# One ring of 24 buffers for weights, late FFN features, q and k and pooled features in a two-layer hybrid trunk, and a queue order at the start

## The chip, the cores and the metric

The kernel runs on one core of one Trainium2 chip. The metric is the device time of one execution in microseconds (us). The engines are PE (TensorE: matmuls, with weight loads as PEld), DVE (VectorE), ACT (ScalarE), POOL (GpSimd) and SP (SyncE, which here only issues DMAs). Each engine works through its own queue in order.

## The reference, cut to what matters

Two layers on x of 512 x 1024 in float32. Each layer is a half-step FFN, a mixer and a second half-step FFN, each followed by a layer norm of the sum with the scaled input. The mixer of layer 0 is an attention of 8 heads, that of layer 1 a pooling mixer.

```python
def swiglu(x, w_gu, w_down):
    g, u = jnp.split(x @ w_gu, 2, axis=-1)
    return (jax.nn.silu(g) * u) @ w_down
...
    for i in range(DEPTH):
        x = layer_norm(DEEPNORM_ALPHA * x + 0.5 * swiglu(x, ffn_w_gu[i, 0], ffn_w_down[i, 0]), ln_g[i, 0], ln_b[i, 0])
...
        x = layer_norm(DEEPNORM_ALPHA * x + y, ln_g[i, 1], ln_b[i, 1])
        x = layer_norm(DEEPNORM_ALPHA * x + 0.5 * swiglu(x, ffn_w_gu[i, 1], ffn_w_down[i, 1]), ln_g[i, 2], ln_b[i, 2])
```

The inner width of an FFN is 2816. So there are six phases: FFN 0, attention, FFN 2, FFN 3, pooling, FFN 5 (the numbers are those of the layer norms behind them).

## The kernel before

Every product is done in three passes on two float32r halves of each operand (`mm3`, L99): high times low, high times high, low times high. `split` (L94) makes the halves: ACT copies the high one (L96), DVE subtracts for the low one (L97). Weights are split too, 458 times 128 x 1024.

The weights flow through one list of pieces and one list of units, written down before the first instruction. A **piece** is a load of 128 x 1024 (4 KB in each partition); a **unit** is one split of a piece. `load` (L179) puts a piece into one of RAW = 7 buffers "raw", with a DMA that SP issues. `prepare` (L192) splits the next unit into one of PARTS = 5 buffers "hi" and one of 5 "lo". `run_ahead` (L203) keeps 5 units prepared beyond those whose matmuls are written, and `load_ahead` (L188) keeps 7 pieces loaded. Both are called by `retire` (L213), which stands behind the matmuls that use a unit.

Most products of an FFN are done by a scheme with seven products in place of eight. A `Quad` (L128) has five pieces, of which two, s1 and s3, are sums of two blocks of weights: SP loads the first block, then POOL issues a DMA that adds the second one (L185). From the seven units of a quad, in the order `LATER` = 1, 2, 6, 5, 7, 3, 4, unit 6 is split from a sum which DVE makes: `sums` (L136) adds s1 to p11 and then p11 to p12 (both L139). Unit 4 of the whole list is the first of the first quad, so unit 6 of the whole list is the first with such a sum.

An FFN begins with four plain units (the first 256 columns of gate and up, L525 to L541): columns of rows 0 to 255 (h = 0) and then of rows 256 to 511 (h = 1). During h = 0, behind the third and the sixth stretch of 12 matmuls (`LATE`, L58), it takes up what is left of the layer norm before (`late`): the tiles t = 2 and t = 3 are transposed on PE (L312), brought from PSUM by ACT or DVE (L315, L323, L321), and split (L255 or L272). Behind h = 0 the input's own sums follow (`Seven.sums`, L282: four of `form`, L279). Then come ten quads jj (L548 to L580), whose gated features go to hT, 22 tiles of 128 x 512; then the down product, first by the same scheme for the features 0 to 7, then plainly (`BProduct`, L413), where `act` (L609) splits the other 14 features of hT in pairs. At the kernel's very start the second of the two `late` steps (L843) also calls `run_ahead`.

A mixer begins with `halves` (L390): blocks of 12 matmuls go through the first halves of up to four pairs of units, then through the second halves.

What sets the order: PE's instructions stay in the order of the program (L87). On the other engines the framework that builds the kernel orders the queues by its own estimate of when each instruction could start; among those that it takes to be ready, the one written first goes first. A buffer of a ring is given out again when its last reader is done.

Of the kernel before, what the change touches and what calls it, by code (L numbers as in the profile page):

```python
# [25 lines left out]
F32 = mybir.dt.float32  # L26
F32R = mybir.dt.float32r
AF = mybir.ActivationFunctionType
ALU = mybir.AluOpType
# [3 lines left out]
P = 128  # L33
S = 512
# [4 lines left out]
NF = FF // P  # L39
# [3 lines left out]
H = 8  # L43
DH = D // H
BUCKETS = 32
# [3 lines left out]
GW = 640  # L49
WINDOWS = (2, 4, 8, 16)  # L50
BLOCK = 8
R = 4
R_LAST = 5
RAW = 7
PARTS = 5
ACT = 7
# [23 lines left out]
def trunk(ctx, tc, x, rel_bias, ln_g, ln_b, w_gu, w_dq, w_down, a_in, a_out, b_in, b_group, b_scale, b_out, onehot, out):  # L80
    nc = tc.nc
# [92 lines left out]
    b_plain(b_out[0], POOL_ORDER)  # L174
    ffn_units(1, 1)

    parts, taken, retired = [], [0], [0]

    def load():  # L179
        p = pieces[len(loaded)]  # L180
        p.tile = wp.tile([P, 1024], F32, tag="raw", bufs=RAW, name=f"raw{len(loaded)}")
        dst = p.tile.rearrange("p (k c) -> p k c", c=p.src.shape[-1]) if len(p.src.shape) == 3 else p.tile
        nc.sync.dma_start(dst, p.src)
        if p.plus is not None:
            nc.gpsimd.dma_start(p.tile, p.plus, accum_op=ALU.add)  # L185
        loaded.append(p)

    def load_ahead():  # L188
        while len(loaded) < len(pieces) and (len(loaded) < RAW or pieces[len(loaded) - RAW].uses == 0):
            load()  # L190

    def prepare():  # L192
        i = len(parts)
        make, done = units[i]
        src = make()
        hi = wp.tile([P, 1024], F32R, tag="hi", bufs=PARTS, name=f"hi{i}")
        lo = wp.tile([P, 1024], F32R, tag="lo", bufs=PARTS, name=f"lo{i}")
        split(hi, lo, src)
        for p in done:
            p.uses -= 1  # L200
        parts.append((hi, lo))

    def run_ahead():  # L203
        load_ahead()
        while len(parts) < min(len(units), retired[0] + PARTS):
            prepare()
            load_ahead()

# [4 lines left out]
    def retire(count=1):  # L213

        retired[0] += count
        run_ahead()
# [44 lines left out]
    class Seven(Plain):  # L261
# [7 lines left out]
        def put(self, t, half, src):  # L269
            c = slice((t % 2) * P, (t % 2 + 1) * P)  # L270
            o = self.operand(((1, 2), (8, 3))[t // 2][half])
            split(o[:, 0, :, c], o[:, 1, :, c], src)  # L272

        def take(self, i, src):
            o = self.operand(i)
# [98 lines left out]
    def load_residual():  # L374
        if residual[0][1] is not None:
            row[:] = ln_params(residual[0][1])
# [93 lines left out]
    gd = dram.tile([H, GW], F32, name="gd")  # L470
    gr = dram.tile([H, P, GW], F32, name="gr")

    def bias_rows(room):

        oh, gs, rb = room[0:BUCKETS, 0:GW], room[0:H, 1024:1024 + GW], room[0:BUCKETS, 2048:2048 + H]
        nc.gpsimd.dma_start(oh, onehot)
        nc.gpsimd.dma_start(rb, rel_bias)
        gp = bank(6, "gp")
        nc.tensor.matmul(gp[:H, :], rb, oh[:, 0:512], start=True, stop=True)
# [13 lines left out]

    def ffn(n, x, dest):
        with tc.tile_pool(name=f"ffn{n}", bufs=1) as fp:
            hT = fp.tile([P, NF, S], F32, name=f"hT{n}")
            kept = {}

            def two(ap):
                return ap.rearrange("p (s c) -> p s c", c=256)  # L500
# [8 lines left out]
            def gate(f, t0, t1, g, u, sign):  # L509
                sg = fp.tile([P, t1 - t0], F32, tag=f"sg{t1 - t0}", bufs=1 if t1 - t0 == S else 2, name=f"sg{n}_{f}_{t0}")  # L510
                nc.scalar.activation(sg, g, AF.Silu, scale=sign)
                return nc.vector.scalar_tensor_tensor(hT[:, f, t0:t1], u, sign, sg, op0=ALU.mult, op1=ALU.mult)

            def product(acc, w, xi, first, last, shared=True):

# [12 lines left out]
            for h, xi in enumerate(((1, 2), (8, 3))):  # L528
                c = slice(h * 256, (h + 1) * 256)
                for i in range(4):  # L530
                    two_accs = [acc[:, c] for acc in accs[i // 2 * 2:i // 2 * 2 + 2]]
                    for _ in product(two_accs, w[i], x.parts[xi[i % 2]], i % 2 == 0, i % 2 == 1, False):
                        if steps in LATE:
                            late.pop(0)()
                        steps += 1
                    if h == 1:
                        if i % 2 == 1:
                            gate(i // 2, 0, S, accs[i - 1], accs[i], 1.0)
                        retire()
                if h == 0:  # L540
                    x.sums()  # L541

# [5 lines left out]
            for jj in QUADS:  # L548
                if n == 0 and jj == 2:
                    columns()  # L550
                if n == 0 and jj == 4:
                    bias_rows(hT[:, 14:22, :].rearrange("p f c -> p (f c)"))
                if jj == 2:
                    load_residual()
                ca = fp.tile([P, 2, S], F32, tag="ca", name=f"ca{n}_{jj}")
                cb = fp.tile([P, 2, 256], F32, tag="cb", name=f"cb{n}_{jj}")
                banks = [bank(i, f"gu{n}_{jj}_{i}") for i in (2 * ((jj + 1) % 3), 2 * ((jj + 1) % 3) + 1, 6 + jj % 2)]
# [51 lines left out]
            def act(f):  # L609
                if f // 2 not in pairs:  # L610
                    two = glob.tile([P, 2, 2, S], F32R, tag="act", bufs=ACT, name=f"h{n}_{f // 2}")
                    split(two[:, 0], two[:, 1], hT[:, f // 2 * 2:f // 2 * 2 + 2, :])
                    pairs[f // 2] = two
                two = pairs[f // 2]
                return two[:, 0, f % 2, :], two[:, 1, f % 2, :]
# [6 lines left out]


    def attention(n, x, dest):
        with tc.tile_pool(name="att", bufs=1) as ap:
            oT, qk, v, probs, pT = {}, {}, {}, {}, {}

            def project(acc, nm, h):
                two = [ap.tile([P, S], F32R, tag=f"{nm}{i}", bufs=2, name=f"{nm}{i}_{h}") for i in range(2)]
                split(two[0], two[1], acc)  # L630
                qk[nm, h] = two

            def values(hp, vp, tt):
                acc = bank(tt, f"v{hp}_{tt}")
# [63 lines left out]
            for hp in range(H // 2):  # L698
# [29 lines left out]
                values(hp, vp, 1)  # L728
                retire(2)
                transposes(h)  # L730
            out_p = BProduct(n, NK, lambda f: (oT[f // 2][:, 0, f % 2, :], oT[f // 2][:, 1, f % 2, :]), 1.0, dest)
            pre = [out_p.take(f) for f in range(NK - R)]
            for t in (1, 0, 3, 2):
# [7 lines left out]


    def pooling(n, x, dest):
        with tc.tile_pool(name="pool", bufs=1) as pp:
            inv = pp.tile([P, 16], F32, name="inv")
            sc = cols[:, 2 * NL:]
# [5 lines left out]
            def pool(acc, cc):  # L752
# [13 lines left out]
                                               op0=ALU.mult, op1=ALU.subtract)  # L766
                g = cc // 2
                if g not in pT:
                    pT[g] = [pp.tile([P, 2, S], F32R, tag=f"pT{i}_{g % 3}", name=f"pT{i}_{g}") for i in range(2)]
                return split(pT[g][0][:, cc % 2, :], pT[g][1][:, cc % 2, :], pl)  # L770

            def group(g, w, b0):
# [38 lines left out]
            def y_of(f):  # L811
                cc = POOL_ORDER[f]
                return yT[cc // 2][:, 0, cc % 2, :], yT[cc // 2][:, 1, cc % 2, :]

            out_p = BProduct(n, NK, y_of, 1.0, dest)
            pre = [out_p.take(f) for f in range(NK - R)]
            for t in range(NT):
# [66 lines left out]
```

## Time and profile before

| | |
|---|---|
| Time before, median of 3 runs | 1738.93 us (1737.85 to 1741.2) |
| The profiled execution, its own time | 1737.85 us |
| Its span, first to last instruction | 1736.1 us |
| PE busy | 1705.0 us (98% of the span) |
| DVE busy, ACT busy | 1251.3 us (72%), 825.6 us (48%) |
| Granted TensorE clock, mean | 0.997 |

The profile is of one execution. In its timeline a row has the start, the length, the engine, the line, the operation, its output and inputs, and in brackets how long the engine had sat idle before it and what ended that. In its list of waits a row says who waited for whom, for how many us in total, how many times, and the longest of these.

### The profile page before, as it was taken

Reading aid. Unit: us, or ns where it says so; the run is one execution under the profiler, and the core shown is the slowest. Engines: PE = TensorE matmul, PEld = TensorE weight load, DVE = VectorE, ACT = ScalarE, POOL = GpSimd, SP = SyncE. Lnnn points to the kernel's source line nnn. Section 1 sums busy time; section 2 is a strip of 40 time slices with the busy share of each in tenths; the row PEclk is TensorE's granted clock in tenths of the full one; section 3 lists DMA queues with packets and bytes.
Section 4 is the critical chain, followed back from the end, with each engine's and each line's share of the span. In section 5 each row is a group of like instructions: output and inputs, shape, how many; then the busy total and the mean of one; then the engine's idle time right before and its main releaser. Section 6 shows DMA issues by size and latency. Waiting matters only on the chain.

```text
span 1736.1 us, 28083 instructions
## 1 busy us (share of the span) xinstructions
PE 1705.0 (98%) x11555; PEld 1585.1 (91%) x11555; DVE 1251.3 (72%) x1657; ACT 825.6 (48%) x1161; POOL 94.5 (5%) x132
## 2 busy tenths in 40 slices
PE   7999999999999999999999999999999999999998
PEld 6999998889888899999888999998888899999886
DVE  5777698266665877878928778788279787877946
ACT  5545464254443555455525554564254454545620
POOL 1010000000000000000000000000000000000000
PEclk9999999999999999999999999999999999999999
DMA  6787756323221376666633666756223356776611
GB/s 209 188 238 186 189 146 209 97 74 110 86 86 51 109 194 176 185 181 164 194 97 85 183 182 185 184 154 197 96 88 106 99 166 187 185 189 180 185 62 49
DMA packets 84864, 257.30 MB, mean 148 GB/s; under 512 B 8128, under 2 KB 25576, under 8 KB 84736
## 3 DMA queue, kind: packets, MB, share of 16 engines
q1 hardware_dynamic: 70080, 202.40, 35.0%
q0 software_dynamic: 14656, 53.12, 17.1%
q8 instruction: 90, 1.47, 0.3%
q14 instruction: 38, 0.31, 0.1%
HBM read 253.37 MB, written 4.74 MB: 149 GB/s over the span
## 4 chain that ended last, share of the span: by engine, by line
PE 93%; DMA 3%; DVE 2%; issue 1%; ACT 0%; SPq 0%; DVEq 0%; POOLq 0%
PE gu L101 16%; PE gu L102 16%; PE gu L103 16%; PE acc L102 8%; PE acc L103 8%; PE acc L101 8%; DMA raw<-in_ffn_w_gu 2%; PE qk L103 2%; PE da L102 2%; PE da L101 2%; PE da L103 2%; PE qk L101 2%; PE qk L102 2%; PE d L102 1%; PE d L103 1%; PE d L101 1%
## 5 line engine op out<-in xcount | busy, mean ns | idle before, releaser
L96 ACT ACTIVATE hi<-raw 128x1024 fp32r<-128x1024 f32 x458 | 484.6, 1061 | 661.4 <-PE gu L102 251.8
L97 DVE TENSOR_TENSOR lo<-raw,hi 128x1024 fp32r<-128x1024 f32 x458 | 557.5, 1222 | 323.6 <-ACT hi L96 322.0
L101 PE MATMUL gu<-x,hi 128*128 128x256 f32 x2496 | 710.3, 285 | 12.4 <-DVE x L97 6.7
L102 PE MATMUL gu<-x,hi 128*128 128x256 f32 x2496 | 707.8, 284 | 0.0
L103 PE MATMUL gu<-x,lo 128*128 128x256 f32 x2496 | 707.7, 284 | 0.0
L101 PEld LDWEIGHTS gu<-x,hi 128*128 128x128 f32 x2496 | 480.7, 193 | 16.6 <-DVE x L97 9.7
L102 PEld LDWEIGHTS gu<-x,hi 128*128 128x128 f32 x2496 | 480.8, 193 | 0.0
L103 PEld LDWEIGHTS gu<-x,lo 128*128 128x128 f32 x2496 | 480.6, 193 | 0.0
L101 PE MATMUL acc<-lo,h 128*128 128x512 f32 x448 | 174.8, 390 | 0.0
L103 PE MATMUL acc<-hi,h 128*128 128x512 f32 x448 | 174.3, 389 | 0.0
L102 PE MATMUL acc<-hi,h 128*128 128x512 f32 x448 | 174.3, 389 | 0.0
L139 DVE TENSOR_TENSOR raw<-raw,raw 128x1024 f32<-128x1024 f32 x96 | 117.5, 1224 | 22.6 <-DMA raw<-in_ffn_w_gu 20.3
L185 POOL DMA_DIRECT2D raw<-in_ffn_w_gu x80 | 69.3, 866 | 1070.0 <-DMA raw<-in_ffn_w_gu 736.4
L103 PEld LDWEIGHTS acc<-hi,h 128*128 128x128 f32 x448 | 84.1, 188 | 17.5
L101 PEld LDWEIGHTS acc<-lo,h 128*128 128x128 f32 x448 | 84.1, 188 | 17.4
L102 PEld LDWEIGHTS acc<-hi,h 128*128 128x128 f32 x448 | 84.1, 188 | 17.1
L507 DVE TENSOR_TENSOR ca<-gu,kept 128x512 f32<-128x512 f32 x80 | 55.2, 691 | 32.3 <-PE gu L103 32.3
L504 ACT ACTIVATE kept<-gu 128x512 f32<-128x512 f32 x120 | 69.5, 580 | 0.0
L323 ACT ACTIVATE st<-tp,cols 128x128 f32<-128x128 f32 x140 | 53.0, 466 | 20.2 <-PE tp L312 20.2
L97 DVE TENSOR_TENSOR x<-st,x 128x512 fp32r<-128x512 f32 (+1 forms) x64 | 51.4, 820 | 15.4 <-ACT x L96 14.8
L101 PE MATMUL qk<-x,hi 128*128 128x512 f32 (+1 forms) x160 | 56.4, 353 | 1.1 <-ACT hi L96 1.0
L103 PE MATMUL qk<-x,lo 128*128 128x512 f32 (+1 forms) x160 | 55.6, 347 | 1.2 <-DVE sm L352 1.2
(155 smaller groups left out, 2101.1 us busy)
## 6 DMA issues: line engine op xcount, KB each, us to landing
raw<-in_ffn_w_gu SPq DMA_DIRECT2D x216, 512.0 KB, 5.8
raw<-in_ffn_w_gu POOLq DMA_DIRECT2D x80, 512.0 KB, 8.3
raw<-in_ffn_w_down SPq DMA_DIRECT2D x56, 512.0 KB, 4.2
raw<-in_ffn_w_dq SPq DMA_DIRECT2D x40, 512.0 KB, 4.0
raw<-in_a_w_in SPq DMA_DIRECT2D x24, 512.0 KB, 3.6
raw<-in_ffn_w_dq POOLq DMA_DIRECT2D x16, 512.0 KB, 5.7
raw<-in_a_w_out SPq DMA_DIRECT2D x8, 512.0 KB, 3.8
raw<-in_b_w_in SPq DMA_DIRECT2D x8, 512.0 KB, 3.5
```

The costliest lines, as they stand in the source:

```text
L96: nc.scalar.activation(hi, src, AF.Copy)
L97: return nc.vector.tensor_tensor(lo, src, hi.bitcast(F32), op=ALU.subtract)
L101: nc.tensor.matmul(acc, sh, ml, start=first, stop=False, skip_group_check=shared)
L102: nc.tensor.matmul(acc, sh, mh, start=False, stop=False, skip_group_check=shared)
L103: nc.tensor.matmul(acc, sl, mh, start=False, stop=last, skip_group_check=shared)
L139: nc.vector.tensor_tensor(d, d, more, op=ALU.add)
L185: nc.gpsimd.dma_start(p.tile, p.plus, accum_op=ALU.add)
L323: nc.scalar.activation(src[:, i, :], tp[:, c], AF.Identity, scale=g, bias=b)
L504: nc.scalar.activation(kept[i, jj], acc, AF.Copy)
L507: nc.vector.tensor_tensor(out, two(acc), two(kept.pop((i, jj))), op=ALU.add)
```

## The change

One ring "slot" of 24 buffers of 4 KB takes the place of "raw" (7), "hi" (5) and "lo" (5). It also holds the features of an FFN from number 8 on (two to a buffer, from when they are written to when `act` has split them), the split q and k of attention (one buffer per head and kind), the split pooled features, and two small tiles for the attention's position bias, which used to lie in unused parts of hT. hT keeps 8 tiles. A count `held` says how many buffers are taken, or soon will be, by what is not weights; `free` is what is then left beyond 7 raw and 5 units. By it `load_ahead` loads up to 9 pieces and `run_ahead` prepares up to 7 units: 9 and 7 with `held` at 0, 7 and 5 from the quad jj = 8 on. The two loads for the position bias move from the start of POOL's queue to the quad jj = 2. In FFN 0, what `retire` gives DVE during h = 1 is queued behind `x.last`, the last subtraction of the input's splits.

```diff
+SLOTS = 24
-        p.tile = wp.tile([P, 1024], F32, tag="raw", bufs=RAW, name=f"raw{len(loaded)}")
+        p.tile = wp.tile([P, 1024], F32, tag="slot", bufs=SLOTS, name=f"raw{len(loaded)}")
...
+    def free():
+        return SLOTS - RAW - 2 * PARTS - held[0]
     def load_ahead():
-        while len(loaded) < len(pieces) and (len(loaded) < RAW or pieces[len(loaded) - RAW].uses == 0):
+        while len(loaded) < len(pieces) and sum(p.uses > 0 for p in loaded[-32:]) < RAW + 2 * (free() > 1):
             load()
...
-        hi = wp.tile([P, 1024], F32R, tag="hi", bufs=PARTS, name=f"hi{i}")
-        lo = wp.tile([P, 1024], F32R, tag="lo", bufs=PARTS, name=f"lo{i}")
+        hi = wp.tile([P, 1024], F32R, tag="slot", bufs=SLOTS, name=f"hi{i}")
+        lo = wp.tile([P, 1024], F32R, tag="slot", bufs=SLOTS, name=f"lo{i}")
...
     def run_ahead():
         load_ahead()
-        while len(parts) < min(len(units), retired[0] + PARTS):
+        while len(parts) < min(len(units), retired[0] + PARTS + max(0, free() - 2) // 2):
...
         def put(self, t, half, src):
...
-            split(o[:, 0, :, c], o[:, 1, :, c], src)
+            self.last = split(o[:, 0, :, c], o[:, 1, :, c], src)
...
-            hT = fp.tile([P, NF, S], F32, name=f"hT{n}")
+            hT = fp.tile([P, BLOCK, S], F32, name=f"hT{n}")
...
+            def room(jj):
+                if 2 * jj >= BLOCK:
+                    later[jj] = wp.tile([P, 2, S], F32, tag="slot", bufs=SLOTS, name=f"hT{n}_{jj}")
+                held[0] = max(0, min(jj + 2, NF // 2) - BLOCK // 2)
...
-                        retire()
+                        with tc.issue_after(x.last.ins) if n == 0 else ExitStack():
+                            retire()
...
                 if n == 0 and jj == 2:
                     columns()
+                    onehots = bias_load()
                 if n == 0 and jj == 4:
-                    bias_rows(hT[:, 14:22, :].rearrange("p f c -> p (f c)"))
+                    bias_rows(*onehots)
...
-                    split(two[:, 0], two[:, 1], hT[:, f // 2 * 2:f // 2 * 2 + 2, :])
+                    split(two[:, 0], two[:, 1], later[f // 2])
+                    held[0] -= 1
...
     def attention(n, x, dest):
+        held[0] = 4
...
-                two = [ap.tile([P, S], F32R, tag=f"{nm}{i}", bufs=2, name=f"{nm}{i}_{h}") for i in range(2)]
+                two = wp.tile([P, 2, S], F32R, tag="slot", bufs=SLOTS, name=f"{nm}{h}")
...
+            held[0] = 0
             out_p = BProduct(n, NK, lambda f: (oT[f // 2][:, 0, f % 2, :], oT[f // 2][:, 1, f % 2, :]), 1.0, dest)
...
     def pooling(n, x, dest):
+        held[0] = 6
...
-                    pT[g] = [pp.tile([P, 2, S], F32R, tag=f"pT{i}_{g % 3}", name=f"pT{i}_{g}") for i in range(2)]
+                    pT[g] = [wp.tile([P, 2, S], F32R, tag="slot", bufs=SLOTS, name=f"pT{i}_{g}") for i in range(2)]
...
+            held[0] = 0
             out_p = BProduct(n, NK, y_of, 1.0, dest)
```

## Rows read from the trace of the kernel before

**Rows 1.** The page, busy time of each engine

```profile
PE 1705.0 (98%) x11555; PEld 1585.1 (91%) x11555; DVE 1251.3 (72%) x1657; ACT 825.6 (48%) x1161; POOL 94.5 (5%) x132
```

**Rows 2.** Waits of PE: who waited for whom, us, times, longest

```profile
PE gu L101 <- DVE x L97: 6.7, 4, 5.7
PE gu L101 <- DVE cb L507: 5.4, 3, 2.8
PE qk L103 <- DVE sm L352: 1.2, 1, 1.2
PE u L103 <- DVE lo L97: 1.1, 1, 1.1
PE qk L101 <- ACT hi L96: 1.0, 1, 1.0
```

**Rows 3.** Waits of DVE and of SP's queue, same columns

```profile
DVE raw L139 <- DMA raw<-in_ffn_w_gu: 20.3, 6, 7.0
...
SPq L183 <- DVE lo L97: 1035.4, 283, 25.1
```

**Rows 4.** Timeline of DVE at the starts of FFN 2, FFN 3 and FFN 5

```profile
627.79 1.23 DVE L139 TENSOR_TENSOR raw<-raw,raw 128x1024 f32<-128x1024 f32 x1 [2.89 <-DMA raw<-in_ffn_w_gu]
...
973.52 1.23 DVE L139 TENSOR_TENSOR raw<-raw,raw 128x1024 f32<-128x1024 f32 x1 [3.94 <-DMA raw<-in_ffn_w_gu]
...
1424.46 1.23 DVE L139 TENSOR_TENSOR raw<-raw,raw 128x1024 f32<-128x1024 f32 x1 [4.84 <-DMA raw<-in_ffn_w_gu]
```

**Rows 5.** The chain that ended last: start, us, what

```profile
20.39 7.95 DMA raw<-in_ffn_w_gu
...
963.84 9.59 DMA raw<-in_ffn_w_gu
...
1397.31 0.12 PE gu L102
...
1409.72 5.60 DMA raw<-in_ffn_w_gu
...
1416.03 8.34 DMA raw<-in_ffn_w_gu
```

**Rows 6.** Timeline of ACT and DVE at the starts of attention and pooling

```profile
363.89 1.09 ACT L96 ACTIVATE hi<-raw 128x1024 fp32r<-128x1024 f32 x1
...
365.36 2.97 ACT L96 ACTIVATE hi<-raw 128x1024 fp32r<-128x1024 f32 x3
...
366.96 1.17 DVE L97 TENSOR_TENSOR lo<-raw,hi 128x1024 fp32r<-128x1024 f32 x1
...
1281.65 1.17 DVE L97 TENSOR_TENSOR lo<-raw,hi 128x1024 fp32r<-128x1024 f32 x1
```

**Rows 7.** Timeline of ACT and DVE at the kernel's start

```profile
22.51 1.09 ACT L315 ACTIVATE st<-tp 128x512 f32<-128x512 f32 x2 [1.90 <-PE tp L312]
23.48 1.15 ACT L96 ACTIVATE x<-st 128x512 fp32r<-128x512 f32 x2
...
28.43 1.23 DVE L139 TENSOR_TENSOR raw<-raw,raw 128x1024 f32<-128x1024 f32 x1 [7.01 <-DMA raw<-in_ffn_w_gu]
29.57 1.22 DVE L279 SCALAR_TENSOR_TENSOR st<-st,st 128x1024 f32<-128x1024 f32 x1
30.71 1.29 DVE L97 TENSOR_TENSOR x<-st,x 128x512 fp32r<-128x512 f32 x2
```

**Rows 8.** Timeline of DVE and PE, layer norm at the start of FFN 5

```profile
1391.57 1.00 DVE L367 TENSOR_SCALAR ax<-ax,sm 128x512 f32<-128x512 f32 x2
...
1392.70 1.03 PE L312 MATMUL tp<-ident,ax 128*128 128x128 f32 x8
```

**Rows 9.** A quad in steady state: timeline of POOL and DVE; DMA issues of the page

```profile
85.95 0.86 POOL L185 DMA_DIRECT2D raw<-in_ffn_w_gu  x1 [15.69 <-DMA raw<-in_ffn_w_gu]
...
96.23 1.22 DVE L139 TENSOR_TENSOR raw<-raw,raw 128x1024 f32<-128x1024 f32 x1
...
raw<-in_ffn_w_gu POOLq DMA_DIRECT2D x80, 512.0 KB, 8.3
```

More of the change, by code (lines that the diff above doesn't have):

```diff
@@ L175, in trunk @@
     ffn_units(1, 1)
-    parts, taken, retired = [], [0], [0]
+    parts, taken, retired, held = [], [0], [0], [0]
     def load():
         p = pieces[len(loaded)]
-        p.tile = wp.tile([P, 1024], F32, tag="raw", bufs=RAW, name=f"raw{len(loaded)}")
+        p.tile = wp.tile([P, 1024], F32, tag="slot", bufs=SLOTS, name=f"raw{len(loaded)}")
         dst = p.tile.rearrange("p (k c) -> p k c", c=p.src.shape[-1]) if len(p.src.shape) == 3 else p.tile
@@ L471, in trunk, with bias_load, bias_rows @@
     gr = dram.tile([H, P, GW], F32, name="gr")
[L473 to L477, printed above, removed]
+    def bias_load():
+        oh = wp.tile([BUCKETS, GW + H], F32, tag="slot", bufs=SLOTS, name="oh")
+        gs = wp.tile([H, GW], F32, tag="slot", bufs=SLOTS, name="gs")
+        nc.gpsimd.dma_start(oh[:, 0:GW], onehot)
+        nc.gpsimd.dma_start(oh[:, GW:], rel_bias)
+        return oh, gs
+    def bias_rows(oh, gs):
         gp = bank(6, "gp")
-        nc.tensor.matmul(gp[:H, :], rb, oh[:, 0:512], start=True, stop=True)
+        nc.tensor.matmul(gp[:H, :], oh[:, GW:], oh[:, 0:512], start=True, stop=True)
         nc.vector.tensor_copy(gs[:, 0:512], gp[:H, :])
@@ L495, in ffn, with features @@
         with tc.tile_pool(name=f"ffn{n}", bufs=1) as fp:
-            hT = fp.tile([P, NF, S], F32, name=f"hT{n}")
-            kept = {}
+            hT = fp.tile([P, BLOCK, S], F32, name=f"hT{n}")
+            later, kept = {}, {}
+            def features(f):
+                return hT[:, f, :] if f < BLOCK else later[f // 2][:, f % 2, :]
+            def room(jj):
+                if 2 * jj >= BLOCK:
+                    later[jj] = wp.tile([P, 2, S], F32, tag="slot", bufs=SLOTS, name=f"hT{n}_{jj}")
+                held[0] = max(0, min(jj + 2, NF // 2) - BLOCK // 2)
             def two(ap):
@@ L511, in gate @@
                 nc.scalar.activation(sg, g, AF.Silu, scale=sign)
-                return nc.vector.scalar_tensor_tensor(hT[:, f, t0:t1], u, sign, sg, op0=ALU.mult, op1=ALU.mult)
+                return nc.vector.scalar_tensor_tensor(features(f)[:, t0:t1], u, sign, sg, op0=ALU.mult, op1=ALU.mult)
             def product(acc, w, xi, first, last, shared=True):
@@ L550, in ffn @@
                     columns()
+                    onehots = bias_load()
                 if n == 0 and jj == 4:
-                    bias_rows(hT[:, 14:22, :].rearrange("p f c -> p (f c)"))
+                    bias_rows(*onehots)
                 if jj == 2:
                     load_residual()
+                room(jj)
                 ca = fp.tile([P, 2, S], F32, tag="ca", name=f"ca{n}_{jj}")
@@ L628, in project @@
             def project(acc, nm, h):
-                two = [ap.tile([P, S], F32R, tag=f"{nm}{i}", bufs=2, name=f"{nm}{i}_{h}") for i in range(2)]
-                split(two[0], two[1], acc)
-                qk[nm, h] = two
+                two = wp.tile([P, 2, S], F32R, tag="slot", bufs=SLOTS, name=f"{nm}{h}")
+                split(two[:, 0], two[:, 1], acc)
+                qk[nm, h] = two[:, 0], two[:, 1]
             def values(hp, vp, tt):
```

## The prediction

> **What bounds the kernel now.** I read the busy times first: PE works for 1705.0 of the span's 1736.1 us [rows 1], so the change can only win from the 31 us in which it stands still, and not all of them: some lie before the first x and weights can be there, and some behind the last matmul. Next PE's own waits [rows 2]: four waits on the split of x (6.7, of which one takes 5.7), three on an eviction of a gated product (5.4), and one each of 1.2, 1.1 and 1.0 at the starts of attention and pooling. The reader is to see that PE hardly waits anywhere else: all of it stands at the starts of phases, and none in the late quads or in the down products. Then I looked for what stands behind them. Before the sums of weights DVE waits six times for the DMA that POOL issues to add the second block [rows 3], 20.3 us in all. Three of the six, at the starts of FFN 2, 3 and 5, take 2.89, 3.94 and 4.84 [rows 4]. They sum to 11.67, and PE's three waits on evictions to 5.4: DVE works in order, the eviction that gives PE its bank back is queued behind the sum, and the first (11.67 - 5.4) / 3 = 2.09 us of each block cost nothing. The fourth, 7.01 us at the kernel's start, holds back the split of x and is PE's 5.7.
>
> **The change, part by part.** *The sums at three FFN starts.* The chain that ended last shows the order before FFN 5's block: the load of s1 takes 5.60 from its issue at 1409.72, the adding DMA follows at 1416.03 and takes 8.34 [rows 5]. It is the s1 of the second quad. Its load is written behind the second plain unit of h = 1, and its buffer, one of 7, comes free only when the first quad's unit 6 is split. With 24 buffers it is written, in all three FFNs, no later than the end of the product before, so ahead of all of h = 0, which is 96 matmuls at 0.12 [rows 5], 11.5 us. The largest block, 4.84, has to shrink by 2.75 to cost PE nothing. So all three waits go: **-5.4**. The bounds are -5.4 and 0; 0 only if the new ring gives that load its buffer late. Next late would be s3, whose load goes out right behind.
>
> *The starts of attention and pooling.* At the start of a phase only one unit is ready, since 4 of the 5 are held by the tail of the product before. Attention needs units 0 and 2 first. Before, the split of unit 1 comes out of ACT first (at 363.89), that of unit 2 only in the run from 365.36, with its low half at 366.96 [rows 6]; PE waits 1.0 and 1.2. With `held` falling to 2 and then 0 in the tail, six or seven units are allowed and some buffers are spare: units 0 and 1 are ready, and unit 2 has buffers before the tail ends. For pooling it is the same with the low half at 1281.65 [rows 6]. I take all of it: **-2.2 and -1.1**. If the buffers came only with the tail's last matmul, unit 2 would have unit 1's old place on ACT, 1.47 earlier (363.89 against 365.36), and some 0.7 of attention's 2.2 would stay, nothing of pooling's 1.1: bound -2.6 for both together.
>
> *The kernel's start.* The new order on DVE covers what `retire` writes during h = 1. But with `held` at 0, free is 24 - 7 - 10 = 7, and (7 - 2) // 2 = 2 more units are prepared; so the `run_ahead` in the second late step writes units 4, 5 and 6. Unit 6 has the first sum. It is now written before that block and outside it; the retirements under the new order write four plain splits. On DVE the first sum already stood ahead of the last splits of x, though it was written after them [rows 7], because it was taken to be ready sooner; nothing in the change makes it ready later. So I expect it to block as before: adding DMA issued at 20.39, 7.95 in flight [rows 5], sum of 1.23 at 28.43. Two terms move. Nine pieces instead of seven are in flight around it, and the nearest row for an adding DMA beside a full SP queue is the 9.59 at 963.84 [rows 5]: +1.64. Behind the sum came a `form` of 1.22 (1.14 until the split of x at 30.71) [rows 7]; now that the sum is written before the forms, the split of x, ready since about 24.6 and written before both, goes first: -1.14. Together **+0.5**. The ends lie far apart. Below: if the sum does end up behind the splits, the whole wait goes, -5.7. Above: the high half of unit 6, ready once the sum is, may go on ACT ahead of the last evictions and splits of x, of 1.09 and 1.15 for two [rows 7]: with that split at 1.09 [rows 6], 28.43 + 1.64 + 1.23 + 1.09 + 1.09 + 0.58 + 0.65 = 34.7 against 31.4, +3.3. I take the value nearest to the order that the rows show.
>
> [...]
>
> *What costs nothing.* The count and shape of splits, sums and matmuls are the same. The two loads for the position bias go from POOL's start to jj = 2 and are read at jj = 4; two quads of 7 x 24 matmuls at 0.12 hide them, and without that cover they would cost one landing, about 8 us by POOL's median of 8.3 [rows 9]. They and the two bias tiles stand in POOL's queue and in the ring ahead of the next adding DMA, at a place where no block in rows 3 is long. Splits made earlier fall into tails in which ACT has room (48% busy [rows 1]).
>
> **The sum.** -5.4 - 2.2 - 1.1 + 0.5 = -8.2, against the profiled execution's own 1737.85, 1.1 below the median of the runs: 1729.6. About 0.2%, or 3.5 us, is what a measurement can tell from no change here; the three runs shown differ by 3.4.
>
> **The rivals.** *The start goes too* (15%). The order on DVE may come out otherwise, since one more weight split stands before the sum. Then -5.7 replaces +0.5: 1723.4. Against it: nothing in the new block names that sum.
>
> *Half of it comes back* (18%). Before FFN 5's h = 1 DVE is packed; the last layer norm ends at 1392.57, and PE's transposes of it start at 1392.70 [rows 8]: 0.13 of room. Unit 6 and its two sums now fall into that stretch. One more 1.22 in front of the norm costs about 1.1 in each of three FFNs, and if 0.7 stays at attention as well, the time is 1729.6 + 3.3 + 0.7 = 1733.6. For it: the three starts are alike. Against it: as many weight splits leave that stretch as enter it, and only the second sum is extra.
>
> *The full ring blocks the late quads* (11%, slower). From jj = 8 on, 7 raw, 10 halves and 7 buffers of features fill all 24, and a load may have to wait for a buffer that matmuls hold, where before it waited for DVE's split alone (283 times, [rows 3]). In steady state the adding DMA is issued at 85.95, lands 8.3 later at some 94.25, and its sum runs at 96.23 [rows 9]: 1.98 of slack, and 2.09 more that cost nothing. A load late by one unit (24 x 0.12 = 2.88) is free; late by two (5.76) it costs 1.69 in each of 3 quads in 4 FFNs, 20.3: 1749.9. The point from which it decides is 4.07 us of lateness. For it: SP issues in order, so one late load holds all behind. Against it: the counts allow no more than 24, and as many loads and units ahead as before.
>
> *The change doesn't do what it says* (6%): the ring's order gives the early loads no buffer, and the time stays near 1738.
>
> **How the numbers follow.** My forecast, with the start still blocked, has 50%. Faster by over 0.2%, below 1735.4: 48 of these 50, the 15, and 13 of the 18, 76%. Within 0.2%: the other 2 and 5, and the 6, 13%. Slower: 11%. The range reaches from 1722, the first rival with a little more from shorter first matmuls after each wait, to 1738, which takes in the second rival with the start at its upper end (1736.4) and the fourth; what it leaves out is the third and the tails.
>
> **What would show it.** Right: PE's wait on the eviction (5.4) gone and those on qk and u gone or under 0.5; DVE's waits before sums down from 20.3 to one of some 8 to 9 at the start; PE's first wait on the split of x still 5 or more, with the sum ahead of it on DVE. The start is wrong if PE goes on near 26 us. The whole is wrong if PE shows new waits in the quads jj = 8 to 10, on evictions behind a blocked sum, or a wait at the transposes of t = 3 at each FFN's start.

## The result and the profile after

The changed kernel took 1727.28 us (median of 6 runs, 1725.47 to 1730.13) beside 1738.84 for the kernel before in the same series (1737.85 to 1741.2): a ratio of 0.9932 [0.9919, 0.9945], 11.6 us less. Run a second time, beside the last experiments, it took 1726.0, ratio 0.9934 [0.9921, 0.9946]. The forecast was 1729.6. It fell within its range, but the terms behind it did not come out one by one. This section shows where they parted.

The profiled execution took 1726.11 us, its span 1724.3: both 11.7 less than before. PE's busy time on the page answers to [rows 1]:

```profile
PE 1700.8 (99%) x11555; PEld 1581.9 (92%) x11555; DVE 1243.8 (72%) x1657; ACT 824.3 (48%) x1161; POOL 94.4 (5%) x132
```

With as many instructions as before, PE is busy for 4.2 us less. PE's idle times, added over the trace, fall from 22.6 to 15.1, by 7.5. So the 11.7 of the span are 7.5 of waiting and 4.2 in which the same matmuls keep PE busy for less time. The second part had no term in the forecast.

Waits of PE after, whole list, and DVE's only wait ahead of a sum of weights (who waited for whom, us, times, longest); it answers to [rows 2, 3]:

```profile
PE tp L316 <- DMA ax<-in_x: 7.3, 2, 3.7
PE gu L102 <- DVE x L98: 5.3, 6, 1.0
PE u L102 <- DVE x L98: 0.8, 1, 0.8
PE qk L102 <- DVE x L98: 0.8, 1, 0.8
PE s L102 <- DVE pr L686: 0.7, 3, 0.2
PE gu L104 <- DVE lo L98: 0.3, 1, 0.3
...
DVE raw L140 <- DMA raw<-in_ffn_w_dq: 2.6, 4, 0.9
```

The reader is to see three things. The evictions (cb) are gone from the list. The wait of 5.7 on the first x is gone as well; of the start there remains one of 0.28, on the low half of a weight. And six waits on the split of x, 5.3 in all, stand where 6.7 stood before. Three of them are new, and three, at t = 3, were there before at 0.33 each. The timeline says which. At the kernel's start DVE now does this (the columns are those of [rows 7]):

```profile
18.83 1.29 DVE L98 TENSOR_TENSOR x<-st,x 128x512 fp32r<-128x512 f32 x2 [0.26 <-ACT x L97]
22.76 1.23 DVE L283 SCALAR_TENSOR_TENSOR st<-st,st 128x1024 f32<-128x1024 f32 x1 [2.64 <-ACT st L319]
23.91 1.29 DVE L98 TENSOR_TENSOR x<-st,x 128x512 fp32r<-128x512 f32 x2
...
31.04 1.22 DVE L98 TENSOR_TENSOR lo<-raw,hi 128x1024 fp32r<-128x1024 f32 x1
...
34.44 1.22 DVE L140 TENSOR_TENSOR raw<-raw,raw 128x1024 f32<-128x1024 f32 x1
...
1371.01 1.22 DVE L98 TENSOR_TENSOR lo<-raw,hi 128x1024 fp32r<-128x1024 f32 x1
...
1372.14 1.00 DVE L371 TENSOR_SCALAR ax<-ax,sm 128x512 f32<-128x512 f32 x2
...
1373.06 0.69 DVE L98 TENSOR_TENSOR x<-st,x 128x512 fp32r<-128x512 f32 x1
...
1373.80 0.19 PEld L102 LDWEIGHTS gu<-x,hi 128*128 128x128 f32 x1 [1.23 <-DVE x L98]
```

The last splits of x run at 23.91, and the first sum only at 34.44, without a wait. Not the sum alone has moved: the first low half of the first quad is the row at 31.04. In the kernel before it stood ahead of the splits of x:

```profile
18.64 1.23 DVE L97 TENSOR_TENSOR lo<-raw,hi 128x1024 fp32r<-128x1024 f32 x1
```

The lower rows of the timeline after are the new waits. A low half of a weight, 1.22, stands ahead of the last step of the layer norm of t = 2 (L371); the split of t = 1 behind it comes late, and PE's matmul at 1373.80 waits 0.81. The same wait is there at the starts of attention (356.63), FFN 2 (580.51), FFN 3 (925.18) and pooling (1270.00). At t = 3 of FFN 2, 3 and 5 (594.95, 939.62, 1388.25) PE waits 0.95 each, before 0.33.

The faster matmuls at the start show in a view of stretches (start and end, length, busy time and instructions of PE, PEld, DVE, ACT and POOL, granted clock, DMA share, GB/s). First the kernel before:

```profile
28.00:31.40 3.40, 0.00 (x0) 0.00 (x0) 2.97 (x4) 0.57 (x1) 0.00 (x0) 0.55 0.22 42
31.40:35.00 3.60, 3.55 (x16) 3.56 (x17) 3.56 (x4) 0.48 (x1) 0.00 (x0) 0.50 0.00 0
```

and the same stretch after:

```profile
31.40:35.00 3.60, 3.60 (x33) 3.60 (x32) 3.60 (x4) 3.57 (x5) 0.86 (x1) 1.00 1.02 237
```

Before, the granted clock fell to 0.50 while PE waited, and stayed there until about 35 (the means: 1.00 from 26 to 28, 0.50 from 30 to 35, 0.92 from 35 to 36): the stretch has 16 matmuls, where it has 33 after (the first few of these began ahead of it). In the timeline of the kernel before, 17 matmuls start from 31.45 to 35.21, in 3.76 us, and from there on one every 0.12. 17 x 0.12 is 2.04, so the wait of 5.67 cost some 1.7 on top of its own length.

### The profile page after: what moved, and what is told of

Same layout as the page of the kernel before. It is cut to its first block, busy times and chain, and to the rows that moved or that the text cites. A ratio compares the mean times of both kernels' runs of the same rounds, so it can differ in the third digit from the quotient of the medians.

```text
span 1724.3 us, 28038 instructions
## 1 busy us (share of the span) xinstructions
PE 1700.8 (99%) x11555; PEld 1581.9 (92%) x11555; DVE 1243.8 (72%) x1657; ACT 824.3 (48%) x1161; POOL 94.4 (5%) x132
## 4 chain that ended last, share of the span: by engine, by line
PE 95%; DVE 4%; DMA 0%; issue 0%; ACT 0%; SPq 0%; DVEq 0%
PE gu L102 17%; PE gu L104 17%; PE gu L103 17%; PE acc L104 7%; PE acc L103 7%; PE acc L102 7%; PE qk L102 2%; PE qk L104 2%; PE qk L103 2%; PE da L102 2%; PE da L103 2%; PE da L104 2%; PE d L102 1%; PE d L104 1%; PE d L103 1%; DVE lo L98 1%
## 5 line engine op out<-in xcount | busy, mean ns | idle before, releaser
L97 ACT ACTIVATE hi<-raw 128x1024 fp32r<-128x1024 f32 x458 | 479.2, 1056 | 365.5 <-DVE lo L98 223.0
L524 DVE TENSOR_TENSOR cb<-gu,kept 128x512 f32<-128x512 f32 x40 | 27.6, 690 | 69.9 <-PE gu L104 69.9
L348 DVE SCALAR_TENSOR_TENSOR ax<-acc,ax 128x512 f32<-128x512 f32 x48 | 33.0, 688 | 55.7 <-PE acc L104 55.3
L528 ACT ACTIVATE sg<-cb 128x256 f32<-128x256 f32 x40 | 16.5, 413 | 93.9 <-DVE cb L524 93.9
```

Source lines behind the costliest of these rows:

```text
L348: nc.vector.scalar_tensor_tensor(r, y, self.scale, r, op0=ALU.mult, op1=ALU.add)
L524: nc.vector.tensor_tensor(out, two(acc), two(kept.pop((i, jj))), op=ALU.add)
```

## The experiments

Twelve kernels were run; the last, e11, is the changed kernel once more. e1 and e2 take the queue order away or add it alone, four take the extras or the ring apart, and the rest follow from what these showed. "Extra" loads and units are those beyond 7 and 5. This table has PE's idle times in the timeline of one profiled run of each kernel, summed by place (us); e5, e7, e10 and e11 follow in words. In it "t = 1" means the wait on the split of t = 1 at the phase starts, with what attention and pooling wait there for q, k and u.

| kernel | start | other evictions | evictions at FFN 2, 3, 5 | t = 1, five starts | t = 3, three FFNs | inside pooling | median |
|---|---|---|---|---|---|---|---|
| before | 5.67 | 0 | 5.43 | 3.54 | 0.99 | 0 | 1738.8 |
| after | 0.28 | 0 | 0 | 4.02 | 2.87 | 0 | 1727.3 |
| e1 no queue block | 0.29 | 2.15 | 0 | 4.02 | 2.90 | 0 | 1729.8 |
| e2 queue block only | 0 | 2.17 | 4.11 | 3.54 | 1.00 | 0 | 1732.8 |
| e3 no extra units | 0.28 | 1.99 | 0 | 4.01 | 2.83 | 3.35 | 1733.5 |
| e4 ring, no extras | 0 | 1.64 | 0 | 4.02 | 1.00 | 3.35 | 1731.4 |
| e6 no extra loads | 0 | 1.99 | 0 | 4.00 | 1.01 | 0 | 1724.8 |
| e8 ring alone | 0 | 2.95 | 0 | 4.01 | 1.00 | 3.83 | 1732.0 |
| e9 halves apart | 6.48 | 0 | 0 | 3.53 | 0.99 | 0 | 1732.7 |
| e12 apart and block | 0 | 0 | 0 | 3.51 | 1.00 | 0 | 1724.4 |

**e1: the change without its queue order.**

```diff
-                        with tc.issue_after(x.last.ins) if n == 0 else ExitStack():
-                            retire()
+                        retire()
```

> The changed kernel without the block that queues DVE's work of FFN 0 behind the last split of x; ring, loads and units ahead as changed. Theory A (the first sum went behind the splits because the deep ring changed the order that the framework estimates, not because of the block; the block holds no sum): PE's wait on the split of x in the first 40 us stays under 0.5 us and the time stays at 1727 (1725 to 1730). Theory B (the block did it): DVE waits some 7 us before its first sum again, PE waits 5 to 6 us on the split of x near 26 us and then runs for 4 us at the lower clock, and the time is 1727.3 + 7.3 = 1734.6 (1732 to 1737).

1729.82, ratio 0.9942 [0.993, 0.9955]. Theory A holds. The start stays as in the change: PE waits 0.29 there. So the new order is not needed for that in the changed kernel. The 2.15 that came in at 237.53, an eviction in the last quad of FFN 0, is taken up below.

**e2: the queue order alone, in the kernel before.**

```diff
-            split(o[:, 0, :, c], o[:, 1, :, c], src)
+            self.last = split(o[:, 0, :, c], o[:, 1, :, c], src)
...
-                        retire()
+                        with tc.issue_after(x.last.ins) if n == 0 else ExitStack():
+                            retire()
```

> The kernel before with that block alone (rings raw, hi and lo as before). Here the first sum is written by a retirement inside the block. Theory A and B both: the sum goes behind the last split of x, the wait of 5.7 us and the 1.8 us that the lower clock costs after it go, 1738.8 - 7.3 = 1731.5 (1729 to 1734), with the three eviction waits of 5.4 us in all still there. Rival C (the adding DMA is only waited for a little later): DVE's wait before the first sum moves behind the splits of x and holds back evictions instead; PE then waits 2 us or more between 36 and 50 us and the time is above 1735.

1732.77, ratio 0.9959 [0.9945, 0.9972]. Time and start are as theory A and B had it. The wait at the start goes here too, and something of rival C comes back, later than it had it. From the lists of waits of this run:

```profile
PE gu L101 <- DVE cb L507: 6.3, 4, 2.2
...
DVE raw L139 <- DMA raw<-in_ffn_w_gu: 16.2, 5, 4.3
```

One eviction wait of 2.17 is new, at 55.23, and behind it the clock is at the lower level (0.55 as the mean from 55.2 to 59); three are those of FFN 2, 3 and 5, now 1.16, 1.30 and 1.65 where they were 0.81, 1.86 and 2.76. The order alone is worth 5.8 (1738.61 to 1732.77) and leaves the FFN starts.

**e3: the change without extra units; e4: without extra units and loads.**

```diff
-        while len(parts) < min(len(units), retired[0] + PARTS + max(0, free() - 2) // 2):
+        while len(parts) < min(len(units), retired[0] + PARTS):
```

and in e4 also

```diff
-... sum(p.uses > 0 for p in loaded[-32:]) < RAW + 2 * (free() > 1):
+... sum(p.uses > 0 for p in loaded[-32:]) < RAW:
```

> The changed kernel with 5 units ahead always (up to 9 loads ahead as changed). Theory D (the new PE waits on splits of x at the starts of phases, five of 0.8 and three of 0.95, come from weight splits that the extra units let DVE and ACT take into the layer norm's stretch): they fall back to 0.1 and 0.33, some 5 us less, 1722 (1720 to 1725), and the three waits on evictions stay away because the load of the second quad's s1 is still written before the FFN begins. Rival E (the extra units were what removed waits on weights): the waits at the starts of attention and pooling (2.2 and 1.1) come back, or evictions wait again, and the time is 1729 or more. No change (1725.5 to 1729) would say that both are small or cancel.

> The changed kernel with 7 loads and 5 units ahead always: one ring of 24, the late features, q and k and pooled features in it, and the queue block, but the counts of before. Theory F (the loads written earlier are what removed the eviction waits): the load of the second quad's s1 is again written behind the second plain unit, the three waits of 5.4 us in all come back, as do 2.2 and 1.1 at the starts of attention and pooling, and the time is that of the queue block alone, 1731.5 (1729 to 1734). Rival G (one common ring alone removes them, since a load then takes any free buffer and need not wait for the split of unit 6): no eviction waits, time 1727 or less.

e3 1733.46, ratio 0.9968 [0.9956, 0.9981]; e4 1731.4, ratio 0.9959 [0.9947, 0.9972]. In both the eviction waits at FFN 2, 3 and 5 stay away and the five of 0.80 stay. So theories D (on the 0.80) and F missed, and the extras are the cause of neither; it lies in the buffers. Rival G had the waits right and the time, 1727 or less, wrong. What both kernels lose is inside pooling: PE waits some 2.98 at about 1302 for a high half on ACT and 0.36 for its low half. The 0.95 at t = 3 goes back to 0.33 in e4, and stays in e3: this points at the extra loads, and e6 below confirms it.

**e8: the ring alone (e4 without the queue order).** The edits of e4 and of e1 together.

> The common ring with as many loads (7) and units (5) ahead as before, and without the new order on DVE at the start. What it has to settle is what moved the first sum of weights behind the splits of x at the kernel's start: the new order alone did it in one run, and the run without it had it moved as well. Theory: the ring alone does, since with 24 buffers no half of a weight is held back and the order of the first quad's splits comes out otherwise: then PE starts its first quad without the wait of 5.7 (a gap under 0.5 ahead of it), and the time is near the 1731.4 of the same ring with the order. Rival: it takes the extra units or loads: the sum then blocks DVE for some 7 us at about 21 to 28, PE waits 5 to 6 for the split of x, goes on at the lower granted clock, and the time is 1731.4 + 7.5 = about 1738.9.

1731.97, ratio 0.9959 [0.9944, 0.9974]. PE starts without a wait: the ring alone moves the first sum. It also has the wait inside pooling; from the list of waits and the view of stretches of this run:

```profile
PE u L102 <- ACT hi L97: 3.0, 1, 3.0
...
PE u L104 <- DVE lo L98: 0.9, 1, 0.9
```

```profile
1302.70:1309.50 6.80, 5.95 (x18) 4.49 (x19) 6.69 (x11) 4.00 (x5) 0.00 (x0) 0.75 0.25 77
```

The unit that pooling needs is split too late when no unit is prepared beyond five, and again the lower clock follows (0.75 is a mean over the stretch). In the kernel before, with 5 + 5 buffers of their own, that wait is not there [rows 2]; nor in e9 below, where the halves have their own buffers too.

**e9: the halves of the weights in their own buffers.** The ring alone, with this edit:

```diff
-SLOTS = 24
+SLOTS = 14
...
-        hi = wp.tile([P, 1024], F32R, tag="slot", bufs=SLOTS, name=f"hi{i}")
-        lo = wp.tile([P, 1024], F32R, tag="slot", bufs=SLOTS, name=f"lo{i}")
+        hi = wp.tile([P, 1024], F32R, tag="hi", bufs=PARTS, name=f"hi{i}")
+        lo = wp.tile([P, 1024], F32R, tag="lo", bufs=PARTS, name=f"lo{i}")
```

> As the run with the ring alone, but the halves of the weights keep their own buffers, 5 each, as before; loaded weights, late features, q and k and pooled features share a ring of 14. It is to settle two things. At the start: theory, it takes loads and halves in one ring to move the first sum, since the order of DVE comes out as before when the halves are apart; then the sum blocks DVE for 6 to 8 us at about 21 to 28, PE waits 4.5 to 6 for the split of x, and the time is some 6 to 7.5 above the 1732.0 of the ring alone, 1738 to 1739.5. Rival: it is the depth of the loads' buffers; then PE starts without that wait and the time is 1732. At FFN 2, 3 and 5: the theory there is that the load of s1 finds a buffer early because loads have more than 7 of them; then the three eviction waits stay away here too (under 0.3 each). If they come back, the halves' buffers were what freed the load, and the time is higher by up to 5.4 more.

1732.67, ratio 0.9969 [0.9956, 0.9981]. Both theories on the mechanisms hold. Waits of PE in this run, whole list, and DVE's wait ahead of a sum:

```profile
PE gu L102 <- DVE x L98: 7.5, 4, 6.5
PE tp L316 <- DMA ax<-in_x: 5.9, 2, 3.5
PE qk L104 <- DVE sm L356: 1.2, 1, 1.2
PE u L104 <- DVE sm L356: 1.1, 1, 1.1
PE qk L102 <- ACT hi L97: 1.0, 1, 1.0
...
DVE raw L140 <- DMA raw<-in_ffn_w_gu: 8.2, 1, 8.2
```

The timeline of POOL and DVE at its start:

```profile
19.14 0.93 POOL L186 DMA_DIRECT2D raw<-in_ffn_w_gu  x1 [15.74 <-DMA raw<-in_ffn_w_gu]
...
28.34 1.23 DVE L140 TENSOR_TENSOR raw<-raw,raw 128x1024 f32<-128x1024 f32 x1 [8.16 <-DMA raw<-in_ffn_w_gu]
29.48 1.22 DVE L283 SCALAR_TENSOR_TENSOR st<-st,st 128x1024 f32<-128x1024 f32 x1
30.62 1.29 DVE L98 TENSOR_TENSOR x<-st,x 128x512 fp32r<-128x512 f32 x2
```

This is the kernel before with one thing mended. The eviction waits of 5.43 are gone, and of DVE's six waits ahead of sums [rows 3] the one at the start is left. The start blocks as the forecast had it; attention and pooling wait as before. The time is 5.8 below 1738.5, where the forecast's term for the three FFN starts was 5.4. That the two are near is in part chance: matmul by matmul, the profile gives 6.2 at these starts, and takes 0.5 back at the kernel's start and 1.5 behind attention's pair of waits, where the granted clock falls in this kernel (last section). The expected total was wrong: 1738 to 1739.5 was worked out from the ring alone, which carries the waits inside pooling and in FFN 0 and FFN 2 that this kernel does not have.

**e12: e9 with the queue order put back.** The edit of e1, the other way round, on e9.

> As the run with the halves apart, with the new order on DVE at the start put back. It tells whether the two causes found add up by themselves: the loads' deeper buffers (which took 5.8 from the time, and all three eviction waits of FFN 2, 3 and 5) and the order of the first sum (PE's wait of 6.48, and the lower granted clock behind it). Theory: they add, so the wait at the start goes, attention and pooling keep their 1.04, 1.19 and 1.06, the waits on x stay at 0.33, and the time is 1732.7 - 6.5 - 1 = about 1725 to 1726, level with the changed kernel without its other parts. Rival: the sum, now behind the splits of x, comes late for the quad that needs it, as in the run of the order alone (an eviction wait of 2.2 near 55 and the lower clock behind it, 4.0 in all); then the time is 1729 to 1730.

1724.43, ratio 0.9924 [0.9911, 0.9938], 8.2 below e9 (7.8 by the two ratios). The two causes add. The first sum still waits on DVE, but behind the splits of x, and nobody waits for it:

```profile
29.09 1.23 DVE L140 TENSOR_TENSOR raw<-raw,raw 128x1024 f32<-128x1024 f32 x1 [2.17 <-DMA raw<-in_ffn_w_gu]
```

The wait near 55 that e2 had is not there.

**e5: a queue order in the tails too.** The change, with

```diff
-            split(hi[:, :, t * P:(t + 1) * P], lo[:, :, t * P:(t + 1) * P], src)
+            self.last = split(hi[:, :, t * P:(t + 1) * P], lo[:, :, t * P:(t + 1) * P], src)
...
-            retire(self.r)
+            with ExitStack() if last else tc.issue_after(self.dest.last.ins):
+                retire(self.r)
```

> The changed kernel with one order added: in the tails of the products of type B the weight split that `retire` writes may not be issued ahead of the split of x of the tile just normalized. What it has to settle is PE's 0.80 at five starts of a phase (356.63, 580.51, 925.18, 1270.00, 1373.80; 4.0 in all), where DVE does a low half of a weight (1.22) ahead of the last step of the layer norm of t = 2 and the split of t = 1. Theory: the place of that one instruction is the cause. Then the five waits fall below 0.2 each, and the time from 1727.3 to about 1723.5. Rival: DVE's stretch as a whole is too full there, and work moved behind is missed later. Then the five may go, but the 0.95 at the three t = 3 (594.95, 939.62, 1388.25) grows by up to 1.2 each, or the gated products wait on evictions again, and the time stays between 1726 and 1729.

1726.34, ratio 0.9928 [0.9915, 0.994]. The 0.80 went from t = 1, so the place of that low half was the cause. But not all of it was won: attention waits 1.36 in place of 0.80, the transposes of t = 3 wait 0.66 for the layer norm in two FFNs, and 0.24 stays at pooling: 2.9 for 4.0 at these places. The 0.95 at the three t = 3 is 0.32, 0.80 and 0.32, and an eviction in FFN 0 waits 0.90. This is nearer to the rival, a stretch of DVE that is nearly full, than to the theory.

**e6: the change without extra loads.** The second edit of e4 alone.

> The changed kernel with at most 7 loads in flight instead of 9, extra units kept. PE's wait of 0.95 at t = 3 of FFN 2, 3 and 5 was 0.94 without the extra units and 0.33 without extra units and loads. Theory: the extra loads are its cause, since the sums that they make ready fall among the splits of the last x. Then the three go to 0.33 here, the five of 0.80 stay, and the time is 1727.3 - 3 x 0.62 = about 1725.4. Rival: it takes either of the two extras to bring it; then the three stay at 0.95 and the time at 1727, or above it if a late load brings back an eviction wait.

1724.8, ratio 0.9919 [0.9906, 0.9931]. The three waits at t = 3 are at 0.33 again, as expected. Beside e4, it differs by the extra units alone: 1724.8 against 1731.4, and the wait inside pooling is gone. So the extra units earn their place in pooling, and the extra loads seem to cost something: 2.3 to 2.6 between e6 and the two series of the change by their ratios, 2.1 between e4 and e3, the same sign twice, with intervals that overlap each time. The profiled executions of e6 and the change do not show it: 1726.17, with 1.99 of waits on evictions, and 1726.11.

**e7: both edits; e10: both, but the order not in the tail ahead of attention.** e10 has, in place of e5's last edit,

```diff
+            with ExitStack() if last or n == 0 else tc.issue_after(self.dest.last.ins):
```

> Both edits before together: the order in the tails, and at most 7 loads in flight. If both theories hold and the gains add, the five waits of 0.80 and 0.62 of each of the three waits of 0.95 go: 1727.3 - 4.0 - 1.9 = about 1721.4. If they compete for the same stretch of DVE, the time is that of the better of the two, about 1723.5; if the rivals hold for both, 1727.

> At most 7 loads in flight, and the order in the tails, but not in the first tail, the one ahead of attention, where that order made PE's wait 1.36 in place of 0.80. Theory: that wait goes back to 0.80 and the rest stays as in the run of both (1724.1): about 1723.5. Rival: the low half that comes back ahead of the layer norm moves what follows in attention as well, and nothing is won: 1724 to 1725. In either case it should be below the changed kernel in the same series of runs, by 3 to 4 (1727.3 before): if it is not, what the traces show of the five and three waits does not reach the time.

e7 took 1724.09, ratio 0.9914 [0.99, 0.9927]; that the gains do not add is the middle case of what was expected. e10 took 1722.8 (1722.03 to 1724.8), ratio 0.9912 [0.9898, 0.9925]: each of its five runs is below each of the five of the change in the same series (1725.02 to 1730.67). Its waits:

```profile
PE tp L316 <- DMA ax<-in_x: 6.4, 2, 3.6
PE tp L316 <- DVE ax L371: 1.3, 2, 0.7
PE qk L102 <- DVE x L98: 0.8, 1, 0.8
PE gu L102 <- DVE x L98: 0.8, 1, 0.8
PE s L102 <- DVE pr L687: 0.7, 3, 0.2
PE u L102 <- DVE x L98: 0.2, 1, 0.2
```

Without the first tiles of x this list has 3.8 us of waits; that of the kernel before had 15.4 [rows 2]. It is the fastest of the kernels run, though e6, e7 and e12 lie within its interval.

**e11: the change once more.**

> The changed kernel itself once more, beside the two above, so that the comparison with the version that is to beat it is made on one chip and in one series. Expected: 1727.3 again, within 1, with the waits at the same places: no wait at the start, none on evictions, 0.80 at five starts of a phase and 0.95 at three t = 3.

1726.0, as said above. Its profiled run was its slowest, 1730.67, and it was not as expected: there is one wait on an eviction. The timeline of DVE and the stretch behind:

```profile
234.12 1.23 DVE L140 TENSOR_TENSOR raw<-raw,raw 128x1024 f32<-128x1024 f32 x1 [3.16 <-DMA raw<-in_ffn_w_dq]
...
237.54 1.22 DVE L140 TENSOR_TENSOR raw<-raw,raw 128x1024 f32<-128x1024 f32 x1
238.67 0.68 DVE L524 TENSOR_TENSOR cb<-gu,kept 128x512 f32<-128x512 f32 x1
```

```profile
239.40:243.00 3.60, 3.59 (x17) 3.59 (x18) 3.16 (x4) 2.82 (x4) 0.00 (x0) 0.53 0.01 1
```

The sum for the down product of FFN 0 waits 3.16 for its adding DMA, the eviction behind it is late, PE waits 2.14, and the matmuls behind it go at the lower clock, 17 of them in 3.6 us. In the first profile of the same kernel the sums at this place wait 0.38 and no eviction waits. This one place, on the edge of being late, is the 2.15 of e1 and may be much of the spread of the change's runs.

## Why the prediction was right, and where its steps failed

**The sums at three FFN starts (-5.4): right.** The waits of 5.43 are gone, in the change and in e9. The reason held as put: s1 finds a buffer early. The adding DMA for the second quad of FFN 5 goes out on POOL at 1416.03 in the kernel before, at 1357.71 in the changed kernel and at 1359.71 in e9, where of the six blocks on DVE only the one at the start is left. It needs no extra loads (e4), and no ring shared with the halves (e9); loads that draw on 14 buffers, shared with the late features, in place of 7 of their own are enough.

**The kernel's start (+0.5): wrong, and the largest error.** The step that failed is "nothing in the change makes it ready later", together with "the run_ahead in the second late step writes units 4, 5 and 6", which followed where unit 6 is written and left out what the buffers do to the order. The rival "the start goes too" had the outcome, but not the reason: it named one more weight split ahead of the sum. e8 has neither that block nor a sixth unit, and the sum moves behind the splits of x all the same; e9 differs by the buffers of the halves, and it blocks. So the common ring changed how the framework orders the queue, before any of the counts that I had followed. Why its estimate falls out so is not settled here. The rival had its price from the wait alone, 5.7; the runs add about 1.7 for the lower clock behind it. Between e9 and e12, where the order makes the same difference, it is some 8.

**The +1.64 on the adding DMA: nearly right in size.** It takes 9.14 in the changed kernel, from 20.36 to 29.50, and 9.10 in e9, where the sum blocks: 1.2 more than 7.95. The traces show more of SP's loads beside it. In the kernel before, SP's last load there landed at 25.95, and POOL's adding DMA at 28.34. The packets by queue (number, MB, share of the engines' time) from 26 to 28.3, in the kernel before:

```profile
q0 software_dynamic: 130, 0.47, 102.6%
```

and in the changed kernel, where q1 is that of SP's loads and seven of them were in flight when the adding DMA was issued, for four before:

```profile
q0 software_dynamic: 80, 0.30, 65.9%
q1 hardware_dynamic: 85, 0.32, 36.9%
```

In this stretch the queue of POOL's adding DMAs moved 80 packets beside 85 of SP's loads, where it had moved 130 without them. The -1.14 beside it no run shows: in e9 a `form` of 1.22, at 29.48, still goes ahead of the split of x at 30.62, but there unit 6 is not written early.

**Attention (-2.2) and pooling (-1.1): too large.** Attention's first waits went from 2.23 to 0.80, pooling's from 1.05 to 0.81. The cause given, "six or seven units are allowed", is not the one: e8 allows five and has the same 0.80. The common ring does it, since e9 has the old waits: in e8 ACT makes no high half of a weight between 351 and 360, around attention's start at 357.64, while e9 makes them at 363.49 and 364.96, ahead of its waits at 366.09 and 367.78, as before. And what is late next had not been named: the split of t = 1.

**"Half of it comes back" (18%): this happened,** beside the forecast and not in place of it. A low half of a weight now stands in front of the layer norm in FFN 2, 3 and 5, as that rival had it. Waits at t = 1 there went from 0.09, 0.09 and 0.07 to 0.80 each, +2.2, and those at t = 3 by +1.9: 4.0 for a price of 3.3. Against it I had said that as many weight splits leave that stretch as enter it; one 1.22 at the wrong place is enough. The rival's reason, units prepared earlier, is not needed for the 0.80: e4 and e8 allow five units and have it too. e5 shows the place, e6 that the t = 3 part belongs to the extra loads.

**The sum, corrected, in us of the profiled span:** FFN starts -5.4; start -5.4 for the wait and -1.7 for its clock; attention -1.4, given back by half inside it (+0.7, three waits of 0.23 ahead of the scores); pooling -0.2; t = 1 and t = 3 of the FFNs +4.0; the first tiles of x +0.4. That is -9.0 of the 11.7. Of the other 2.7, 2.5 lie in PE's busy time (4.2 less the 1.7 at the start). Set side by side matmul by matmul, 1.3 of them lie in the first 15 us: matmuls start every 0.21 until 14.66 before, and until 12.03 after. That is no gain of the change: in e11, the same kernel, they do so until 14.03. About 1 more lies at the waits themselves, 0.26 net for each that goes: 0.10 behind it, where the first matmul takes 0.22 to the next start in place of 0.12, and 0.16 ahead of it, where a matmul of 0.28 runs to its end (so around the wait that ends at 1428.73 in the kernel before). The forecast was 8.2 to the measured 11.6, and that it came so near was luck: an error of -7.6 at the start and errors of +6.4 in attention, pooling and the FFN starts nearly cancelled.

**The full ring (11%) did not come, but its sign did.** In the first profile of the change, quads jj = 8 to 10 show no new wait. In e11, the same kernel, the last quad of FFN 0 has one on an eviction behind a blocked sum, 2.14, as that rival had it. Apart from e2's, all waits under "other evictions" in the table are in the last quad of an FFN, and only kernels with the common ring have them. A load late for want of a buffer is not behind e11's: its adding DMA goes out at 225.03, where the first profile has 224.03, and then takes 9.00 in place of 5.97. SP's loads do wait for matmuls now, which the rival needed (142 times for the matmuls of gate and up); no wait of PE is traced to that, and the landings are shorter at the median. DMA issues of the page after, beside the 8.3 of [rows 9]:

```profile
raw<-in_ffn_w_gu SPq DMA_DIRECT2D x216, 512.0 KB, 4.0
raw<-in_ffn_w_gu POOLq DMA_DIRECT2D x80, 512.0 KB, 6.6
```

## What to carry to other kernels

Give each stream of buffers the depth that its own waits ask for before merging rings: deeper buffers for loads and one queue order (e12) gave 13 of the 16 us that the best version here gave, with the halves of the weights in buffers of their own, and the ring that takes them in (e8) brought waits of its own. A change of buffers also reorders the queues that a framework sorts, so compare the order of each in-order engine at the phase starts, not only the counts. Price a wait of PE with what may follow it: the lower clock cost 1.7 behind the 5.67 at the start, and as much behind waits of 2.14 (e11, 0.53 over 3.6 us) and 2.17 (e2, 0.55 over 3.8 us).

## What the runs showed of the hardware that I had not expected

In these runs a wait of PE did not need to be long for the granted clock to fall behind it, and its length alone did not decide. It fell behind 2.14 (e11, mean 0.53) and 2.17 (e2, 0.55), but not behind 2.15 in e1, at the same place of the program as e11's, nor behind the 2.76 that ends at 1428.73 in the kernel before (1.00 from there to 1432). The stretch behind e1's wait, beside the 0.53 of e11 above:

```profile
237.53:241.13 3.60, 3.60 (x27) 3.51 (x28) 3.17 (x4) 3.37 (x5) 0.00 (x0) 1.00 0.00 0
```

It fell behind the pair of 1.04 and 1.19 at the start of attention in e9, and in e2 (0.60) and e12 (0.63) as well, but not behind the same pair in the kernel before. The stretch right behind the pair, in the kernel before:

```profile
368.20:372.00 3.80, 3.80 (x32) 3.80 (x33) 3.69 (x8) 0.67 (x4) 0.00 (x0) 1.00 0.92 270
```

and in e9:

```profile
368.00:372.00 4.00, 4.00 (x23) 4.00 (x23) 3.57 (x8) 0.03 (x1) 0.00 (x0) 0.60 0.88 289
```

23 matmuls in 4.0 us, against 32 in 3.8. What decides between the two is left open by these runs; it makes a wait of some 2 us cost either 2 (the 2.15 of e1) or about 4 (the 2.14 of e11 and some 1.7 behind it).

POOL's adding DMAs moved half as much per us as SP's loads, with the DMA engines as busy. Two stretches of the kernel before, the first with SP's loads alone, the second with POOL's adding DMAs alone (last columns: share of the engines, GB/s):

```profile
18.00:20.00 2.00, 2.00 (x19) 2.00 (x18) 1.81 (x2) 2.00 (x5) 0.00 (x0) 1.00 1.02 406
26.00:28.30 2.30, 0.00 (x0) 0.00 (x0) 0.00 (x0) 0.00 (x0) 0.00 (x0) 1.00 1.03 203
```

The share of the engines is 1.02 at 406 GB/s and 1.03 at 203 GB/s.
